# All of w_down's product by seven products: z's factors kept split in DRAM, and some weights' rests made by adding DMAs

## The chip, the cores and the metric

The kernel runs on one core of a Trainium2 chip. The metric is device microseconds (us) of one execution. The kernel before was timed three times: median 1957.88 us, 1957.66 to 1958.37. TensorE (PE) multiplies into PSUM banks; VectorE (DVE), ScalarE (ACT) and GpSimd (POOL) do the rest; SyncE (SP) issues most of the DMAs, ACT's queue some.

## The reference

One layer of a hybrid streaming encoder, 512 positions of 2048 channels, float32:

```python
u = rms_norm(h, mix_pre_gain)
p = u @ w_in                      # 2048 x 5120, two convolution branches follow
o = concat(y_a, y_b) @ w_out      # 2048 x 2048
h = h + rms_norm(o, mix_post_gain)
m = rms_norm(h, mlp_pre_gain)
z = square(relu(m @ w_up))        # 2048 x 8192
z = z @ w_down                    # 8192 x 2048
h = h + rms_norm(z, mlp_post_gain)
```

The change touches the last two products, the MLP.

## The kernel before

**Precision.** A float32 operand is split into a high part (rounded to fp32r by ACT) and a rest (value minus high part, by DVE). A product of two such operands takes three matmuls: high x rest, rest x high, high x high.

**Products by seven.** A 2 x 2 block product is made from seven block products instead of eight, with sums of blocks on either side (Strassen's scheme in Winograd's form). In the code `r11`, `r21`, `r22` are plain blocks of the activation side, `t1` to `t4` sums of them; on the weight side `n11`, `n12`, `n21`, `n22` are blocks and `s1` to `s4` sums, made on DVE from freshly loaded raw weights.

**Weights.** The class `Stationary` (lines 109 to 254) keeps an ordered list of jobs, one for each 128 x 1024 piece. A job loads raw pieces on SP's queue into 6 `raw` buffers, adds or subtracts where it is a sum, then makes the high part (line 237, ACT) and the rest (line 242, DVE) into two of 43 `slot` buffers of 4 KB a partition, which most things share; the oldest free one is taken. `take(n, ahead)` prepares jobs `ahead` of the ones used. Raw loads are issued in order when a job that frees a raw buffer is done, `W.ahead` = 5 sources further on.

**The first MLP product** (lines 766 to 860): eight of the 64 output tiles of w_up plainly, then 28 pairs of tiles by `by_seven` (line 361). Each of a pair's seven products has 24 matmuls of 256 columns into a bank of its own, of seven that rotate. Work on the result is put in `pending` and issued in the next product, behind the preparation of weights (`run_pending` after `W.take`). After a pair, ACT makes Relu and Square and stores z to DRAM (`relu_squared`, line 766).

**The second MLP product** (lines 863 to 1019): w_down's 64 row blocks in eight chunks of eight, the result in column tiles of 512. z is the stationary side (128 x 128 blocks), weights move, 512 columns a matmul (`wide`, lines 882 to 884). In each of seven chunks, two column tiles are made plainly (`wide_tile`, four token banks of 8 blocks each) and two by seven (`wide_seven`), their results added up in SBUF by DVE (line 335, through `accumulate`). z comes back from DRAM and is split there; for the sums it is loaded again, subtracted and split (`strassen_sums`). The last chunk is made plainly for all four tiles, its second half by token block at the end, so that the norm's sums and the output follow block by block. There `turn` transposes h back on PE (line 999).

The order of work is written out by hand: each engine issues in program order, and waits are semaphores that follow from the data and from the reuse of buffers.

## Time and profile before

| | |
|---|---|
| median of three runs | 1957.88 us |
| profiled execution | 1959.29 us, its span 1957.6 us |
| busy: PE, DVE, ACT, POOL | 99%, 78%, 42%, 4% |
| first MLP product by sevens, in the window 750 to 1277 us | PE busy throughout, DVE 403.56 of 527 us |
| w_down product, in the window 1420 to 1856 us | PE busy throughout, DVE 346.57 of 436 us |
| DMA over the span | 272.54 MB, 139 GB/s |

The span goes from the first to the last instruction. Busy time is the union of an engine's instructions; matmuls are pipelined, so the duration of one is longer than the step from one to the next. Rows of groups show line, engine, operation, output and inputs by the program's names, shape and count, then busy us and mean ns, then the idle time before them and what ended it.

### The profile page before, as it was taken

What the parts mean: (1) busy time and instruction counts of PE and PEld (TensorE: products, weight loads), DVE (VectorE), ACT (ScalarE), POOL (GpSimd) and SP (SyncE); (2) the same over time, 40 slices, a digit from 0 to 9 for tenths busy, and PEclk for the clock granted to TensorE, in tenths of its full rate; (3) what the DMA queues carried; (4) which work ended last, traced back from release to release, by engine and by line L of the source; (5) the groups of instructions that cost most, each with busy time, mean ns of one, the idle gap of its engine ahead of it and who ended that gap; (6) DMA issues with size and microseconds to landing.
All of it is one profiled execution on the core that took longest, in us unless ns stands there. A gap on an engine that the chain in (4) does not pass through costs nothing.

```text
span 1957.6 us, 28019 instructions
## 1 busy us (share of the span) xinstructions
PE 1936.3 (99%) x11218; PEld 1716.1 (88%) x11218; DVE 1522.6 (78%) x2000; ACT 815.9 (42%) x1102; POOL 75.4 (4%) x70
## 2 busy tenths in 40 slices
PE   8999999999999999999999999999999999999998
PEld 6888888888999789999999999988888888888876
DVE  8799989667785787777777777776687777877748
ACT  6222112252443745454444545446243343433442
POOL 4000010300210000000000000000000000000000
PEclk9999999999999999999999999999999999999999
DMA  7232323232346724343343434446253363533632
GB/s 250 83 113 95 108 87 108 86 107 76 117 153 227 253 81 159 111 137 133 116 155 108 158 112 135 147 171 235 84 197 130 129 219 102 195 127 132 237 107 87
DMA packets 85523, 272.54 MB, mean 139 GB/s; under 512 B 9616, under 2 KB 11792, under 8 KB 85392
## 3 DMA queue, kind: packets, MB, share of 16 engines
q1 hardware_dynamic: 71568, 245.92, 38.1%
q10 hardware_dynamic: 13824, 24.82, 3.3%
q8 instruction: 88, 1.44, 0.3%
q14 instruction: 43, 0.35, 0.1%
HBM read 241.87 MB, written 28.84 MB: 138 GB/s over the span
## 4 chain that ended last, share of the span: by engine, by line
PE 96%; DVE 2%; DMA 1%; ACT 1%; issue 0%; SPq 0%; ACTq 0%; DVEq 0%
PE bank L296 57%; PE bank L882 11%; PE bank L883 11%; PE bank L884 11%; PE bank L315 2%; PE bank L316 2%; PE bank L314 2%; DVE slot L242 1%; DMA tmp<-x_in 1%; PE bank L999 0%; DVE slot L98 0%; PE sums L383 0%; DVE slot L1077 0%; DMA raw<-w_in_in 0%; DMA par_sb<-par_in 0%
## 5 line engine op out<-in xcount | busy, mean ns | idle before, releaser
L296 PE MATMUL bank<-slot,slot 128*128 128x256 f32 (+1 forms) x7584 | 1127.6, 311 | 0.0
L296 PEld LDWEIGHTS bank<-slot,slot 128*128 128x128 f32 x7584 | 1047.0, 191 | 80.1 <-issue 1.4
L242 DVE TENSOR_TENSOR slot<-raw,slot 128x1024 fp32r<-128x1024 f32 x332 | 410.6, 1255 | 61.7 <-ACT slot L237 55.4
L237 ACT ACTIVATE slot<-raw 128x1024 fp32r<-128x1024 f32 x332 | 338.1, 1049 | 134.0 <-DVE raw L212 67.4
L882 PE MATMUL bank<-slot,slot 128*128 128x512 f32 x968 | 378.1, 391 | 0.8
L883 PE MATMUL bank<-slot,slot 128*128 128x512 f32 x968 | 376.7, 389 | 0.2 <-DVE slot L95 0.2
L884 PE MATMUL bank<-slot,slot 128*128 128x512 f32 x968 | 376.7, 389 | 0.0
L237 ACT ACTIVATE slot<-slot 128x1024 fp32r<-128x1024 f32 x170 | 176.9, 1057 | 285.3 <-PE bank L296 161.7
L242 DVE TENSOR_TENSOR slot<-slot,slot 128x1024 fp32r<-128x1024 f32 x170 | 210.7, 1240 | 56.9 <-PE bank L882 41.8
L882 PEld LDWEIGHTS bank<-slot,slot 128*128 128x128 f32 x968 | 181.7, 188 | 40.8 <-ACT tmp L1002 3.3
L883 PEld LDWEIGHTS bank<-slot,slot 128*128 128x128 f32 x968 | 181.7, 188 | 37.8 <-DVE slot L95 0.5
L884 PEld LDWEIGHTS bank<-slot,slot 128*128 128x128 f32 x968 | 181.7, 188 | 37.8
L335 DVE TENSOR_TENSOR tmp<-tmp,bank 128x256 f32<-128x256 f32 x224 | 93.9, 419 | 113.5 <-PE bank L296 112.4
L94 ACT ACTIVATE slot<-tmp 128x512 fp32r<-128x512 f32 x96 | 54.1, 607 | 274.1 <-DVE tmp L335 153.4
L501 DVE SCALAR_TENSOR_TENSOR slot<-slot,par_sb,slot 128x512 f32<-128x512 f32 x240 | 163.0, 746 | 0.0
L335 DVE TENSOR_TENSOR slot<-slot,bank 128x512 f32<-128x512 f32 x164 | 105.8, 682 | 19.1 <-PE bank L884 19.1
L95 DVE TENSOR_TENSOR slot<-slot,slot 128x512 fp32r<-128x512 f32 (+1 forms) x80 | 49.7, 660 | 48.4 <-ACT slot L94 48.4
L314 PE MATMUL bank<-slot,slot 128*128 128x512 f32 (+1 forms) x216 | 81.1, 375 | 6.2 <-ACT slot L94 6.2
L316 PE MATMUL bank<-slot,slot 128*128 128x512 f32 (+1 forms) x216 | 81.0, 375 | 2.9 <-DVE slot L98 2.9
L95 DVE TENSOR_TENSOR slot<-tmp,slot 128x512 fp32r<-128x512 f32 x96 | 60.3, 666 | 29.6 <-ACT slot L94 29.4
L315 PE MATMUL bank<-slot,slot 128*128 128x512 f32 (+1 forms) x216 | 80.9, 374 | 1.8 <-DVE slot L242 1.8
L165 DVE TENSOR_TENSOR slot<-raw,raw 128x1024 f32<-128x1024 f32 x64 | 78.0, 1219 | 0.0
(98 smaller groups left out, 936.4 us busy)
## 6 DMA issues: line engine op xcount, KB each, us to landing
raw<-w_up_in SPq DMA_DIRECT2D x128, 512.0 KB, 5.2
raw<-w_down_in SPq DMA_DIRECT2D x128, 512.0 KB, 4.6
raw<-w_in_in SPq DMA_DIRECT2D x76, 512.0 KB, 4.4
slot<-z_dram SPq DMA_DIRECT2D x60, 512.0 KB, 6.5
raw<-w_out_in SPq DMA_DIRECT2D x32, 512.0 KB, 4.3
z_dram<-tmp ACTq DMA_DIRECT2D x64, 256.0 KB, 5.4
tmp<-x_in SPq DMA_DIRECT2D x16, 256.0 KB, 5.2
slot<-x_in SPq DMA_DIRECT2D x8, 512.0 KB, 8.7
```

Source lines behind the costliest of these rows:

```text
L95: nc.vector.tensor_tensor(lo, value, hi.bitcast(F32), op=ALU.subtract)
L237: nc.scalar.activation(hi, value, AF.Copy)
L242: nc.vector.tensor_tensor(lo, value, hi.bitcast(F32), op=ALU.subtract)
L296: nc.tensor.matmul(ps, s, m, start=n == 0, stop=n == len(todo) - 1)
L314: nc.tensor.matmul(ps[:, cols], hi, mhi, start=first, stop=False)
L315: nc.tensor.matmul(ps[:, cols], lo, mhi, start=False, stop=False)
L316: nc.tensor.matmul(ps[:, cols], hi, mlo, start=False, stop=last)
L335: add = lambda out, a, b, op=ALU.add: nc.vector.tensor_tensor(out, a, b, op=op)
L501: nc.vector.scalar_tensor_tensor(out=acc, in0=g[:, k : k + S], scalar=w, in1=acc, op0=ALU.mult, op1=ALU.add)
L882: nc.tensor.matmul(ps, z_hi, lo, start=first, stop=False)
L883: nc.tensor.matmul(ps, z_lo, hi, start=False, stop=False)
L884: nc.tensor.matmul(ps, z_hi, hi, start=False, stop=last)
```

## The change

All four column tiles of w_down's product are now made by seven in each of the seven chunks, two `wide_seven` calls a chunk in place of two plain tiles and one call. Products that share a term go on in the same PSUM bank: the three of `p6`, the two of `p5` and the two of `p1` each have a pair of banks, which DVE reads between them. What belongs to three of the four quarters (`p1`) is added up once in `shared` and put into them near the end.

z's parts and sums are made in the first product, by steps (`z_jobs`) of which one goes along with each product (two where more than eight wait): Relu, Square and high part; store and rest; store and the sums t1 to t4; their high part; store and rest; store. Parts lie in DRAM by factor, so that the second product loads ready factors (`load_factor`) and splits nothing. Stores have rows of 1 KB, four a partition; a factor's load has rows of 4 KB.

`by_seven` makes its products in the order r11, t2, t1, r21, t3, r22, t4; r21 goes on in r11's bank and t4 in t3's, with a sign turned in t4. DVE makes five additions a pair instead of seven, and ACT one more copy.

One weight piece a pair in w_up and two a unit in w_down get their rest without DVE: ACT writes the negated high part, and a DMA that POOL issues adds the raw weights to it from DRAM. w_down's units load in another order, their `12` pieces into slots.

The diff at its core ("..." where lines are left out; removed lines are shown only in `prepare`, `product` and `by_seven`):

```diff
+            self.jobs.append((lambda: self.get(n), n + 1, None))
+        def strassen(self, even, odd, added_up=False):
+            def sub(out, a, b, op=ALU.subtract):
+                nc.vector.tensor_tensor(out, a, b, op=op)
+                return out
             def p6():
+                s["1"], s["2"] = slot([P, WCOLS]), slot([P, WCOLS])
+                sub(s["1"], self.get(n21), self.get(n22), ALU.add)
+                return sub(s["2"], s["1"], self.get(n11))
+            def p7():
+                return sub(self.get(n11), self.get(n11), self.get(n21))
+            for value, frees, added in (
+                (lambda: self.get(n11), 0, None),
+                (p6, 0, None),
+                (lambda: s["1"], 0, None),
+                (lambda: self.get(n12), 0, None),
+                (p7, 2, None),
+                (lambda: sub(s["2"], self.get(n12), s["2"]), 0, None),
+                (lambda: self.get(n22), 4, odd[1] if added_up else None),
+                self.jobs.append((value, n11 + frees if frees else 0, added))
...
         def strassen_wide(self, units):
+            n, s, last = {}, {}, {}
+            for name in ("21a", "22a", "21b", "22b", "11a", "11b"):
                 n[name] = self.source(units[name])
+            first = n["21a"]
...
             def raw(name):
+                return self.get(n[name])
             def s1(u):
                 s[u] = slot([P, WCOLS])
+                return sub(s[u], raw("21" + u), raw("22" + u), ALU.add)
             def s2(u):
+                last[u] = slot([P, WCOLS])
+                nc.sync.dma_start(last[u], units["12" + u])
+                return sub(s[u], s[u], raw("11" + u))
+            for value, frees, added in (
+                (lambda: s1("a"), 0, None),
+                (lambda: s1("b"), 0, None),
+                (lambda: s2("a"), 0, None),
+                (lambda: s2("b"), 0, None),
+                (lambda: raw("11a"), 0, None),
+                (lambda: raw("11b"), 0, None),
+                (lambda: sub(raw("11a"), raw("11a"), raw("21a")), 2, None),
+                (lambda: sub(raw("11b"), raw("11b"), raw("21b")), 4, None),
+                (lambda: sub(s["a"], last["a"], s["a"]), 0, None),
+                (lambda: sub(s["b"], last["b"], s["b"]), 0, None),
+                (lambda: raw("22a"), 5, units["22a"]),
+                (lambda: raw("22b"), 6, units["22b"]),
+                (lambda: last["a"], 0, None),
+                (lambda: last["b"], 0, None),
+                self.jobs.append((value, first + frees if frees else 0, added))
...
         def prepare(self, upto):
             while len(self.parts) < upto:
                 while len(self.high) < min(len(self.parts) + 2, len(self.jobs)):
-                    value = self.jobs[len(self.high)][0]()
+                    value, _, added = self.jobs[len(self.high)]
+                    value = value()
                     hi, lo = slot([P, WCOLS], F32R), None
                     nc.scalar.activation(hi, value, AF.Copy)
+                    if added is not None:
+                        lo = slot([P, WCOLS], F32R)
+                        nc.scalar.activation(lo, hi.bitcast(F32), AF.Copy, scale=-1.0)
+                        nc.gpsimd.dma_start(lo, added, accum_op=ALU.add)
                     self.high.append((value, hi, lo))
                 value, hi, lo = self.high[len(self.parts)]
                 if lo is None:
                     lo = slot([P, WCOLS], F32R)
-                nc.vector.tensor_tensor(lo, value, hi.bitcast(F32), op=ALU.subtract)
+                    nc.vector.tensor_tensor(lo, value, hi.bitcast(F32), op=ALU.subtract)
...
     for m in range(UP_PLAIN, N_UP, 2):
+        W.strassen(w_up[m], w_up[m + 1], True)
     for c in range(N_CHUNK - 1):
+        for _ in range(N_WIDE // 2):
+            W.strassen_wide({name: w_down[next(down_units)] for name in SEVEN_UNITS})
+    def products(ps, blocks, at=None, f=None, onto=False):
...
+            nc.tensor.matmul(
+                ps, s, m, start=n == 0 and not onto, stop=n == len(todo) - 1, skip_group_check=onto
+            )
...
-    def product(right, blocks):
+    def product(right, blocks, onto=None):
         (part,) = W.take(1, 3)
         run_pending()
-        ps = bank(TOK)
-        products(ps, [(block(part, i), right(i)) for i in range(blocks)])
+        ps = bank(TOK) if onto is None else onto
+        products(ps, [(block(part, i), right(i)) for i in range(blocks)], onto=onto is not None)
         return ps
     def by_seven(product, c1, c2, done1, done2, step=lambda n: None):
-        p1, u = scratch(TOK), scratch(TOK)
-        evacuate(nc.scalar.activation, p1, product("r11"), AF.Copy)
+        p1, u, v = scratch(TOK), scratch(TOK), scratch(TOK)
+        first = product("r11")
+        evacuate(nc.scalar.activation, p1, first, AF.Copy)
         evacuate(add, u, p1, product("t2"))
-        p5 = product("t1")
-        evacuate(add, c1[:, upper], u, p5)
-        evacuate(add, c1[:, lower], p1, product("r21"))
-        evacuate(add, u, u, product("t3"))
-        evacuate(add, c2[:, upper], u, p5)
+        evacuate(add, v, u, product("t1"))
+        product("r21", first)
+        evacuate(nc.scalar.activation, c1[:, lower], first, AF.Copy)
+        seventh = product("t3")
+        evacuate(add, c2[:, upper], v, seventh)
         evacuate(step, 1)
-        evacuate(add, c2[:, lower], u, product("t4"), ALU.subtract)
+        evacuate(add, c1[:, upper], v, product("r22"))
+        evacuate(done1, c1)
+        evacuate(step, 3)
+        product("t4", seventh)
+        evacuate(add, c2[:, lower], u, seventh)
         evacuate(done2, c2)
-        evacuate(step, 3)
-        evacuate(add, c1[:, upper], c1[:, upper], product("r22"))
-        evacuate(done1, c1)
...
+    FACTORS = ("r11", "r12", "r21", "r22", "t1", "t3", "t2", "t4")
+    WIDE_ORDER = ("t1", "t2", "r11", "t3", "r22", "t4", "r21")
+    PAIRS = CHUNK // 2
+    z_dram = dram.tile([P, N_UP // 2 * 16 * TOK], F32, name="z_dram")
+    z_parts = z_dram.rearrange(
+        "p (c g f h i w) -> c g h i p f w", g=2, f=4, h=2, i=PAIRS, w=TOK
+    )
+    z_jobs = deque()
+    def keep_z(n, zt):
+        c, i = divmod(n, PAIRS)
+        made = {}
+        def squared():
+            nc.scalar.activation(zt, zt, AF.Relu)
+            nc.scalar.activation(zt, zt, AF.Square)
+            high(zt, 0)
+        def high(value, g):
+            made["hi", g] = slot([P, 4, TOK], F32R)
+            nc.scalar.activation(
+                made["hi", g].rearrange("p f w -> p (f w)"),
+                value.rearrange("p a b -> p (a b)"), AF.Copy,
+            )
+        def rest(value, g):
+            made["lo", g] = slot([P, 4, TOK], F32R)
+            add(
+                made["lo", g].rearrange("p f w -> p (f w)"),
+                value.rearrange("p a b -> p (a b)"),
+                made["hi", g].rearrange("p f w -> p (f w)").bitcast(F32), ALU.subtract,
+            )
+        def store(g, h):
+            part = made["lo" if h else "hi", g]
+            nc.scalar.dma_start(z_parts[c, g, h, i], part.bitcast(F32))
+        def sums():
+            t = made["t"] = slot([P, 4, TOK])
+            q = zt.rearrange("p a (b w) -> p (a b) w", b=2)
+            add(t[:, :2, :], q[:, 1::2, :], q[:, :2, :], ALU.subtract)
+            add(t[:, 2, :], q[:, 3, :], t[:, 0, :], ALU.subtract)
+            add(t[:, 3, :], q[:, 2, :], t[:, 2, :], ALU.subtract)
+        z_jobs.append([squared])
+        z_jobs.append([lambda: store(0, 0), lambda: rest(zt, 0)])
+        if c == N_CHUNK - 1:
+            z_jobs.append([lambda: store(0, 1)])
+            return
+        z_jobs.append([lambda: store(0, 1), sums])
+        z_jobs.append([lambda: high(made["t"], 1)])
+        z_jobs.append([lambda: store(1, 0), lambda: rest(made["t"], 1)])
+        z_jobs.append([lambda: store(1, 1)])
+    def z_job(n):
+        for _ in range(min(n, len(z_jobs))):
+            pending.extend(z_jobs.popleft())
...
+    def plain_z(n, pss, zt):
+        for i, ps in enumerate(pss):
+            nc.scalar.activation(zt[:, i, :], ps, AF.Copy)
+        keep_z(n, zt)
...
+    def up_product(name, onto=None):
+        z_job(2 if len(z_jobs) > 8 else 1)
+        return product(right_factor[name], HALF, onto)
+    factors = {}
+    def load_factor(c, name):
+        f = FACTORS.index(name)
+        for h in range(2):
+            t = factors[c, name, h] = slot([P, PAIRS, TOK], F32R)
+            nc.sync.dma_start(
+                t.rearrange("p i w -> p (i w)").bitcast(F32),
+                z_dram.rearrange("p (n w) -> n p w", w=PAIRS * TOK)[((c * 2 + f // 4) * 4 + f % 4) * 2 + h],
+            )
+    def load_first(n):
+        for name in WIDE_ORDER[3 * (n == 3) : 3 + (n == 3)]:
+            load_factor(0, name)
...
     for m in range(UP_PLAIN, N_UP, 2):
+        zt = slot([P, 2, S])
         by_seven(
             up_product,
+            zt[:, 0, :],
+            zt[:, 1, :],
+            lambda c: None,
+            lambda c, m=m, zt=zt: keep_z(m // 2, zt),
+            load_first if m == N_UP - 2 else lambda n: None,
+        )
+    total, shared = {}, {}
...
+    def right_blocks(c, name, i):
+        return [factors[c, name, h][:, i, :] for h in range(2)]
...
+    def wide_seven(c, t, after):
+        if c == 0:
+            for name in ((t, 0), (t, 1), (t + 1, 0), (t + 1, 1), None):
+                pair = slot([P, 2, WIDE])
+                if name is None:
+                    shared[t] = pair
+                else:
+                    for j in range(2):
+                        total[name[0], 2 * name[1] + j] = pair[:, j, :]
...
+        banks = {}
+        for q, (name, group, to, first) in enumerate((
+            ("t1", "p5", "c2 upper", True),
+            ("t2", "p6", "c1 upper", True),
+            ("r11", "p1", "all but c1 lower", True),
+            ("t3", "p6", "c2 upper", False),
+            ("r22", "p5", "c1 upper", False),
+            ("t4", "p6", "c2 lower", True),
+            ("r21", "p1", "c1 lower", True),
+        )):
+            z_job(1)
+            parts = W.take(2, 4)
+            run_pending()
+            if group not in banks:
+                banks[group], onto = [bank() for _ in range(2)], False
+            else:
+                onto = True
+            for j, ps in enumerate(banks[group]):
+                for i in range(PAIRS):
+                    wide(
+                        ps, right_blocks(c, name, i), j, parts[i // 2], i % 2,
+                        i == 0 and not onto, i == PAIRS - 1, True,
+                    )
+                evacuate(accumulate, c == 0 and first, sums[to][j], ps)
+            after(q)
+    run_pending()
+    for name in WIDE_ORDER[4:]:
+        load_factor(0, name)
+    for c in range(N_CHUNK - 1):
+        following = WIDE_ORDER if c < N_CHUNK - 2 else FACTORS[:4]
+        def after(q):
+            if q > 0 and q - 1 < len(following):
+                load_factor(c + 1, following[q - 1])
+        for t in range(0, N_WIDE, 2):
+            wide_seven(c, t, after if t == 2 else lambda q: None)
+        if len(following) == len(WIDE_ORDER):
+            load_factor(c + 1, following[-1])
...
```

More of the change, by code (lines that the diff above doesn't have):

```diff
@@ L870, in accumulate @@
             add(to, to, ps)
-    def new_total(t):
-        for n in range(TB // 2):
-            pair = slot([P, 2, WIDE])
-            for i in range(2):
-                total[t, 2 * n + i] = pair[:, i, :]
-    def wide(ps, z_hi, z_lo, part, n, first, last):
-        hi, lo = (w[:, n * WIDE : (n + 1) * WIDE] for w in part)
-        nc.tensor.matmul(ps, z_hi, lo, start=first, stop=False)
-        nc.tensor.matmul(ps, z_lo, hi, start=False, stop=False)
-        nc.tensor.matmul(ps, z_hi, hi, start=False, stop=last)
@@ L886, in encoder_block, with wide @@
-    tokens = lambda n: slice(n * P, (n + 1) * P)
-    def wide_tile(t, first_sum, blocks, make_moving, step=lambda: None, ahead=4):
+    tokens = lambda n: slice(n * P, (n + 1) * P)
+    def wide(ps, right, b, part, n, first, last, onto=False):
+        hi, lo = (w[:, n * WIDE : (n + 1) * WIDE] for w in part)
+        z_hi, z_lo = (t[:, tokens(b)] for t in right)
+        matmul = lambda a, b, first=False, last=False: nc.tensor.matmul(
+            ps, a, b, start=first, stop=last, skip_group_check=onto
+        )
+        matmul(z_hi, lo, first=first)
+        matmul(z_lo, hi)
+        matmul(z_hi, hi, last=last)
@@ L890, in wide_tile @@
+    def wide_tile(t, c, blocks, step):
         pss = [bank() for _ in range(TB)]
         for n in range(0, len(blocks), 2):
-            (part,) = W.take(1, ahead)
+            (part,) = W.take(1, 4)
             run_pending()
             for i in range(2):
-                moving = make_moving(blocks[n + i])
                 for b, ps in enumerate(pss):
                     wide(
-                        ps, *both(moving, tokens(b)), part, i,
+                        ps, plain_block(c, blocks[n + i], b), b % 2, part, i,
@@ L902, in wide_tile @@
         for b, ps in enumerate(pss):
-            evacuate(accumulate, first_sum, total[t, b], ps)
-    def wide_seven(c):
-        if c == 0:
-            for _ in range(7):
-                seven.append(slot([P, 2, WIDE]))
-        for q, name in enumerate(("r10", "t10", "t11", "t20", "t21", "r21", "r20")):
-            parts = W.take(2, 4)
-            run_pending()
-            n, half = int(name[1]) - 1, int(name[2]) * TB // 2
-            right = lambda i: z[c * CHUNK + 2 * i + n] if name[0] == "r" else t_z[i][n]
-            for j in range(2):
-                ps = bank()
-                for i in range(CHUNK // 2):
-                    wide(
-                        ps, *both(right(i), tokens(half + j)), parts[i // 2], i % 2,
-                        i == 0, i == CHUNK // 2 - 1,
-                    )
-                evacuate(accumulate, c == 0, seven[q][:, j, :], ps)
-            if q > 1:
-                z_step(3)
```

177 lines of the change are left out of this document (36 added, 141 removed).

## Prediction

> **What bounds the kernel now.** I read the page's busy times, then TensorE's waits, then the stages.
>
> ```profile
> PE 1936.3 (99%) x11218; PEld 1716.1 (88%) x11218; DVE 1522.6 (78%) x2000; ACT 815.9 (42%) x1102; POOL 75.4 (4%) x70
> PE 96%; DVE 2%; DMA 1%; ACT 1%; issue 0%; SPq 0%; ACTq 0%; DVEq 0%
> ```
>
> ```profile
> PE bank L314 <- ACT slot L94: 6.2, 1, 6.2
> PE bank L316 <- DVE slot L98: 2.9, 4, 0.9
> PE bank L315 <- DVE slot L242: 1.8, 1, 1.8
> PE bank L883 <- DVE slot L95: 0.2, 1, 0.2
> ```
>
> TensorE (PE) is busy for 99% of the span, makes 96% of the chain that ended last, and waits about 11 us in all, nearly all of it ahead of the MLP. Time therefore goes where matmuls go, as long as the other engines keep up. How near they are is read by stage: first the h stage, then the first MLP product by sevens, then the w_down product. Columns: window, its us, then busy us of PE, PEld, DVE, ACT, POOL, the granted clock, the DMA engines' share, GB/s.
>
> ```profile
> 610.00:671.00 61.00, 58.13 (x358) 51.89 (x358) 49.48 (x89) 34.19 (x56) 0.00 (x0) 1.00 0.72 254
> 750.00:1277.00 527.00, 527.00 (x4394) 527.00 (x4393) 403.56 (x469) 254.06 (x312) 0.00 (x0) 1.00 0.41 135
> 1420.00:1856.00 436.00, 436.00 (x1925) 361.04 (x1924) 346.57 (x453) 167.67 (x207) 0.62 (x2) 1.00 0.47 161
> ```
>
> In both stages that the change rewrites PE never idles and VectorE (DVE) is busy for 77% and 79%. It is the engine that could take over.
>
> **Term 1, matmuls removed.** The w_down product's first and last step, the transposes between, and two equal points of successive pairs in the first MLP product:
>
> ```profile
> L882 PE MATMUL bank<-slot,slot x968: 389/389/501, 1279.5 to 1947.3; 128*128 128x512 f32 x194
> L999 PE MATMUL bank<-tmp,slot 128*128 128x128 f32 x64 | 8.3, 272 | 0.0
> 1000.38 0.37 ACT L343 ACTIVATE tmp<-bank 128x256 f32<-128x256 f32 x1
> 1020.53 0.36 ACT L343 ACTIVATE tmp<-bank 128x256 f32<-128x256 f32 x1
> ```
>
> Lines 882 to 884 have 968 each, 2904 in all, so from the first to the last start there are 2903 steps. (667.8 - 8.3) / 2903 = 0.227 us a matmul; the 0.389 us are a pipelined duration, and taking them would overstate the gain. A chunk before: two wide tiles of 8 blocks x 4 token banks x 3 = 192, and seven products of 2 banks x 4 blocks x 3 = 168; together 360. After: 2 x 168 = 336. 24 fewer in each of seven chunks are 168, x 0.227 = **-38.2 us**. The first product keeps 168 matmuls a pair, 20.15 us a pair, 2.88 us for each of its seven products; a product of the second takes 24 x 0.227 = 5.45 us.
>
> **Term 2, the first product's 28 pairs.** They hide all the new z work, so the cover has to be counted. Groups of this stage, and others of the page for single forms:
>
> ```profile
> L242 DVE TENSOR_TENSOR slot<-slot,slot 128x1024 fp32r<-128x1024 f32 x103 | 125.5, 1219 | 0.0
> L335 DVE TENSOR_TENSOR tmp<-tmp,bank 128x256 f32<-128x256 f32 x184 | 77.3, 420 | 106.7 <-PE bank L296 105.8
> L335 DVE TENSOR_TENSOR tmp<-slot,slot 128x512 f32<-128x512 f32 x16 | 11.1, 692 | 0.8
> L237 ACT ACTIVATE slot<-raw 128x1024 fp32r<-128x1024 f32 x80 | 83.8, 1049 | 12.4 <-PE bank L296 12.4
> L343 ACT ACTIVATE tmp<-bank x32: 360/364/366, 520.1 to 1262.5; 128x256 f32<-128x256 f32 x32
> L769 ACT ACTIVATE tmp<-tmp 128x512 f32<-128x512 f32 x52 | 32.9, 633 | 1.7
> 998.98 0.33 ACTq L770 DMA_DIRECT2D z_dram<-tmp  x1
> ```
>
> DVE before, a pair: 11 operations of 1024 (7 rests, 4 sums) x 1.22 + 7 evacuations x 0.42 = 16.4; the window shows 403.56 / 26.15 pairs = 15.4, since neighbours overlap (factor 0.94). After: 10 x 1.22 + 5 x 0.42 for weights and banks, 2 x 1.22 for z's rests, 0.69 + 2 x 0.42 for its sums: 18.3, x 0.94 = 17.2 of 20.15 us (85%). ScalarE (ACT): 254.06 / 26.15 = 9.7, plus a negated copy 1.05, a bank copy 0.36, two z copies 2.10, Relu and Square on 1024 for 512 (-0.4), two more DMA issues 0.7: 13.5 us (67%). Neither exceeds PE, so the base case costs nothing, but DVE's idle time falls from 4.7 to 2.9 us a pair.
>
> Two new waits lie inside. The fourth product goes on in the first's bank after ACT has copied it, with two products (5.8 us) in between. The seventh goes on in the fifth's bank, and DVE must have read that within one product, 2.88 us. Behind the third product's evacuation DVE has z's sums (1.5), two weight sums and two rests (4 x 1.22), then this read: 0.4 + 1.5 + 4.9 + 0.4 = 7.2 us after the third product's end; the seventh starts 3 x 2.88 = 8.6 after it. Margin 1.4 us: enough, if nothing ahead of that read waits.
>
> What can wait is a slot. The right factors hold 28 of the 43, and a pair takes 22 from the other 15, so one is reused one to two products after its release. A z part is released by its store's landing. DMA rows, KB and median us to landing, then the z stores' and z loads' spread:
>
> ```profile
> raw<-w_up_in SPq DMA_DIRECT2D x128, 512.0 KB, 5.2
> raw<-w_down_in SPq DMA_DIRECT2D x128, 512.0 KB, 4.6
> z_dram<-tmp ACTq DMA_DIRECT2D x64, 256.0 KB, 5.4
> slot<-x_in SPq DMA_DIRECT2D x8, 512.0 KB, 8.7
> raw<-w_in_in SPq DMA_DIRECT2D x16, 128.0 KB, 4.0
> DMA to landing us min/median/max: 2.0/5.5/9.4
> GB/s 424 416 414 360 212 113 301 185 395 419 338 21 11 0 0 0 0 67 274 124 277 336 376 359 398 416 407 403 402 306 290 201 211 317 226 285 215 298 185 172
> ```
>
> By my count the next write into the first rest's slot comes about 5.2 us after its store starts. Landing at 5.4 costs nothing beyond the margin; at 9.4 it costs 9.4 - 5.2 - 1.4 = 2.8 us a pair, 78 us. The bytes argue for the near end: nine transfers of 0.524 MB a pair are 4.72 MB in 20.15 us, 234 GB/s, against 5 x 0.524 = 130 before, and the h stage reached 424. A store with rows of 1 KB isn't in the trace; the w_in pieces with such rows (4.0 us for a quarter of the bytes) put it between 4 and 16 us, nearest to 6. I take **+3 us** (0 to 60).
>
> At the stage's start the eight plain tiles leave four pairs of z, 24 z steps, worked off two to a product: the first pair's DVE gets 14 steps for 6, 14 / 6 x 3.7 + 13.5 + 8 late rests x 0.42 = 25.5 us against 20.15. Weights made three products ahead (8.6 us) cover most of it: **+2 us** (0 to 9).
>
> **Term 3, the adding DMAs.** One a pair, two a w_down unit; no such DMA and no DMA from POOL is in the trace, and POOL has nothing else to do there (0.00 above). The hi copy and its negation are issued in the third product, the rest is needed by the seventh: 4 x 2.88 = 11.5 us, less two copies, leaves 9.4 for the landing. Bounds: 5.2 (the same bytes loaded) and 10.4 (source and destination each cost a load). I take 7, nearer to the plain load, and so **0 us** (0 to 28 x 1.0 = 28). In w_down three products, 16.4 us, lie between. What it spares is one DVE rest, in term 2 already. Without it DVE would be at 91%.
>
> While POOL works, a DVE subtract of 1.22 us can take twice as long:
>
> ```profile
> 27.03 2.32 DVE L242 TENSOR_TENSOR slot<-raw,slot 128x1024 fp32r<-128x1024 f32 x1
> 26.40 1.87 POOL L408 TENSOR_TENSOR sum<-sum,tmp 128x512 f32<-128x512 f32 x1 [1.71 <-ACT tmp L412]
> ```
>
> At 1.1 us a DMA this would be 1.1 of DVE's 2.9 idle us a pair, still hidden. [...]
>
> **Term 4, the w_down product.** DVE before, a chunk (360 x 0.227 = 81.8 us of PE):
>
> ```profile
> L335 DVE TENSOR_TENSOR slot<-slot,bank 128x512 f32<-128x512 f32 x120 | 77.2, 683 | 12.3 <-PE bank L884 12.3
> L95 DVE TENSOR_TENSOR slot<-slot,slot 128x512 fp32r<-128x512 f32 x48 | 31.0, 687 | 25.1 <-ACT slot L94 25.1
> SPq L122 <- DVE raw L212: 236.4, 14, 30.0
> ```
>
> 30 weight operations x 1.22, 22 bank additions x 0.68, z's 16 rests x 0.69 and 16 sums x 0.42: 69 us, the window shows 65. After: 40 x 1.22 + 28 x 0.68 = 67.8, x 0.94 = 64 of 76.3 us (84%). Bytes: 20 weight transfers and 14 factors are 17.8 MB, 234 GB/s. SP issues 30 DMAs a chunk for 24, in one order; loads wait there for buffers already (236 us), and a factor that waits for PE now holds back the weights queued behind it. The last raw load of a unit (11b) is asked for only when its sum is next, so DVE waits a load of 4.6 us once a unit, of its 6.2 idle us there. Weights are ready about two products (10.9 us) ahead. **+3 us** (0 to 42, rival 3). A bank is gone on with one product after its read is due, as before by rotation: nothing.
>
> **Term 5, the seam.**
>
> ```profile
> 1269.76 9.64 PE L296 MATMUL bank<-slot,slot 128*128 128x256 f32 x79
> 1279.45 0.50 PE L882 MATMUL bank<-slot,slot 128*128 128x512 f32 x1
> ```
>
> PE passes from one product to the other without a gap. After, it needs two factors whose loads are issued around the last pair's sixth product, behind at most a few raws: **+1 us** (0 to 6). The end (12 additions for 14) changes nothing that PE waits for.
>
> **Sum.** -38.2 + 3 + 2 + 0 + 3 + 1 = -29.2. The span of 1957.6 becomes 1928.4. The profiled execution took 1959.29, 1.4 above the median of 1957.88; on the median the forecast is **1928.7 us**.
>
> **Rivals.** (1) *Stores hold the slots.* If a z store lands at 7.5 us, DVE's fifth-bank read is late by 7.5 - 5.2 - 1.4 = 0.9 us, and PE waits in each pair: 28 x 0.9 = 25 in place of term 2's 3, 1951 us. For it: no slot is spare, DVE at 85%. Against: z stores of half the size land at 5.4, with DMA engines far from full. (2) *Slower: the adding DMA is late* in the first product. Every us beyond 9.4 costs 28; it undoes the gain from 9.4 + 38.2 / 28 = 10.8 us on. At 12, 73 us: 1928.7 + 73 = 2002 us. For it: it must read and write the same bytes. Against: four products of cover. (3) *The SP queue starves w_down.* A factor waiting one product (5.45) ahead of 11b makes DVE's wait 10; less 6.2 idle and some of the lead, 3 us a unit, 14 units, 42: 1968 us. For it: SP's long waits now. Against: PE never waited through them.
>
> **Chances.** Forecast, PE bound with under 20 us of waits: 57%, own range 1918 to 1940. Rival 1: 18%, rival 2: 15%, rival 3: 10%. 0.2%, about what this measurement can tell, is 4 us. Faster: 57 + 13 of rival 1 + 3 of rival 3 = 73%; same: 5 + 2 = 7%; slower: 15 + 5 = 20%. The range runs from all covers holding and the seam free, 1916, to rival 3, 1970.
>
> **What would show it.** 2736 wide matmuls at 0.227 us; pairs still 20.15 us apart; DVE about 85% in both stages; z stores landing under 6.6 us and adding DMAs under 9.4. It is wrong if PE's waits name the bank line in the first product with ACT or DVE or a POOL DMA behind it, or the wide matmuls with a weight's rest behind it, for over 20 us.

## The result: 3.7% slower

The changed kernel takes 2029.84 us (median of four runs, 2024.50 to 2034.29), the kernel before 1957.77 us beside it: ratio 1.0365, 95% interval 1.0352 to 1.0378. The forecast of 1928.7 us and its range, up to 1970, are missed, and with them the sign. The profiled execution took 2024.5 us with a span of 2022.8, so the span grew by 65.2 us.

From the page after, the busy times:

```profile
PE 1919.6 (95%) x11050; PEld 1696.6 (84%) x11050; DVE 1563.1 (77%) x1932; ACT 914.3 (45%) x1114; POOL 129.6 (6%) x126
```

PE makes 168 matmuls fewer, as planned, but idles for 2022.8 - 1919.6 = 103 us, 21 before. Its busy time fell by 16.7 us only: taking away 38.2 leaves 21.5 us by which the remaining matmuls keep it busy longer. DVE, at 77%, is no busier than it was (78%). So no engine ran out of time; PE stands and waits. PE's waits after (waiting line, what released it; us in total, times, longest us):

```profile
PE bank L299 <- DMA slot<-w_up_in: 33.6, 24, 2.6
PE bank L299 <- ACT slot L237: 15.1, 2, 10.0
PE bank L299 <- DVE slot L340: 13.8, 2, 12.5
PE bank L935 <- DVE slot L340: 11.6, 5, 2.9
PE bank L935 <- ACT slot L925: 4.9, 1, 4.9
PE bank L299 <- ACT tmp L348: 2.0, 1, 2.0
```

Line 299 is the first MLP product, line 935 the wide matmuls of w_down; a slot filled from `w_up_in` by a DMA is a rest made by adding (line 241). Line 299 waiting for ACT, DVE and POOL's DMA, for over 20 us, is what the prediction had named as its refutation. By stage, first the first MLP product before, then after (window, its us, busy us of PE, PEld, DVE, ACT and POOL, granted clock, DMA share, GB/s), then after's wide matmuls with their first and last start:

```profile
671.00:1279.50 608.50, 608.45 (x4899) 600.71 (x4897) 462.20 (x561) 298.60 (x381) 0.00 (x0) 1.00 0.40 133
```

```profile
671.00:1358.40 687.40, 622.93 (x4892) 609.86 (x4891) 518.09 (x622) 383.31 (x434) 24.50 (x28) 0.97 0.69 205
```

```profile
L935 PE MATMUL bank<-slot,slot x2736: 387/389/792, 1358.4 to 2013.6; 128*128 128x512 f32 x196
```

The first product takes 78.9 us more. The w_down product takes 655.2 us from its first to its last start, 667.8 before: 12.6 less, that is -38.2 for its removed matmuls and +25.6 of new loss. What follows the last matmul is 1.1 us shorter. 78.9 - 12.6 - 1.1 = 65.2.

**The first product splits once more.** PE's timeline after, stretches without a stop: start, us, and at the end in brackets the stop ahead of the stretch and its releaser. A pair's seven products are 168 matmuls, 20.15 us when undisturbed:

```profile
745.28 22.49 PE L299 MATMUL bank<-slot,slot 128*128 128x256 f32 x168 [12.45 <-DVE slot L340]
777.74 21.76 PE L299 MATMUL bank<-slot,slot 128*128 128x256 f32 x169 [9.97 <-ACT slot L237]
825.57 23.10 PE L299 MATMUL bank<-slot,slot 128*128 128x256 f32 x168 [5.09 <-ACT slot L237]
872.07 20.42 PE L299 MATMUL bank<-slot,slot 128*128 128x256 f32 x168 [1.59 <-DMA slot<-w_up_in]
916.16 21.91 PE L299 MATMUL bank<-slot,slot 128*128 128x256 f32 x168 [1.94 <-DMA slot<-w_up_in]
...
1310.70 20.42 PE L299 MATMUL bank<-slot,slot 128*128 128x256 f32 x168 [2.63 <-DMA slot<-w_up_in]
...
1354.05 4.49 PE L299 MATMUL bank<-slot,slot 128*128 128x256 f32 x23 [2.02 <-DMA slot<-w_up_in]
```

From 872.07 to 1354.05 are 22 pairs of 21.91 us: 1.76 more than before in each, 38.7 in all, with one stop a pair on the adding DMA. The other 40 us lie in the pairs ahead of these, in long stops on ACT and DVE and in slow stretches behind them (granted clock 0.80 from 745 to 757 us, 0.72 from 825 to 837).

**How a steady pair stops.** The timeline around the third product of one pair:

```profile
1099.16 1.05 ACT L790 ACTIVATE slot<-slot 128x1024 f32<-128x1024 f32 x1
1100.24 1.06 ACT L791 ACTIVATE slot<-slot 128x1024 f32<-128x1024 f32 x1
1101.34 1.06 ACT L796 ACTIVATE slot<-slot 128x1024 fp32r<-128x1024 f32 x1
1102.30 1.04 ACT L237 ACTIVATE slot<-raw 128x1024 fp32r<-128x1024 f32 x1
1103.38 1.06 ACT L240 ACTIVATE slot<-slot 128x1024 fp32r<-128x1024 f32 x1
1104.85 0.86 POOL L241 DMA_DIRECT2D slot<-w_up_in  x1 [20.84 <-DVE slot L340]
1105.42 1.22 DVE L163 TENSOR_TENSOR slot<-raw,raw 128x1024 f32<-128x1024 f32 x1
...
1110.39 0.41 DVE L340 TENSOR_TENSOR slot<-tmp,bank 128x256 f32<-128x256 f32 x1
...
1113.45 2.78 PE L299 MATMUL bank<-slot,slot 128*128 128x256 f32 x21 [1.31 <-DMA slot<-w_up_in]
```

The seventh product was due at 1113.45 - 1.31 = 1112.14, so the third began 4 x 2.88 earlier, at 1100.6. But the copy of the last weight (line 237) comes only at 1102.30: ACT has z's Relu, Square and high part (lines 790, 791, 796) ahead of it in its order. POOL issues at 1104.85, which leaves 7.3 us to 1112.14. (The bracket of POOL's row names a DVE operation that ended shortly before; but in each of the last 20 pairs POOL issues 0.41 us after the end of the negated copy, line 240, whatever DVE did, so that copy is what it follows.) The DMA groups of the page (count, KB, median us to landing):

```profile
raw<-w_up_in SPq DMA_DIRECT2D x128, 512.0 KB, 4.5
z_dram<-slot ACTq DMA_DIRECT2D x120, 512.0 KB, 5.9
slot<-w_up_in POOLq DMA_DIRECT2D x28, 512.0 KB, 8.6
slot<-w_down_in POOLq DMA_DIRECT2D x28, 512.0 KB, 8.5
```

8.6 against 7.3 is the 1.3 us by which PE stands.

**How a w_down unit stops.** SP's, DVE's and PE's rows around the end of one chunk, then DVE's wait over seven chunks:

```profile
1540.62 78.11 PE L935 MATMUL bank<-slot,slot 128*128 128x512 f32 x336 [2.87 <-DVE slot L340]
...
1590.20 1.23 SPq L900 DMA_DIRECT2D slot<-z_dram  x2
1591.52 0.38 SPq L207 DMA_DIRECT2D slot<-w_down_in  x1
1591.95 0.42 SPq L122 DMA_DIRECT2D raw<-w_down_in  x1
1600.89 1.23 DVE L195 TENSOR_TENSOR slot<-slot,raw 128x1024 f32<-128x1024 f32 x1 [8.22 <-DMA raw<-w_down_in]
...
1620.38 76.58 PE L935 MATMUL bank<-slot,slot 128*128 128x512 f32 x336 [1.66 <-DVE slot L340]
```

```profile
DVE slot L195 <- DMA raw<-w_down_in: 63.7, 14, 9.4
```

DVE waits 8.22 us for 11b, which SP asked for at 1591.95 behind two factors and another piece. Later in the chunk it reads a bank late (line 340), and PE stops. A chunk takes 1620.38 - 1540.62 = 79.8 us instead of 76.3.

### The profile page after: what moved, and what is told of

Its sections match the earlier page's. It is cut to its first block, busy times and chain, and to the rows that moved or that the text cites. A ratio compares the mean times of both kernels' runs of the same rounds, so it can differ in the third digit from the quotient of the medians.

```text
span 2022.8 us, 28179 instructions
## 1 busy us (share of the span) xinstructions
PE 1919.6 (95%) x11050; PEld 1696.6 (84%) x11050; DVE 1563.1 (77%) x1932; ACT 914.3 (45%) x1114; POOL 129.6 (6%) x126
## 4 chain that ended last, share of the span: by engine, by line
PE 29%; DMA 16%; DVE 8%; issue 6%; ACT 4%; SPq 0%; ACTq 0%; DVEq 0%; POOLq 0%
PE bank L935 24%; DMA z_dram<-slot 7%; DMA slot<-w_up_in 6%; PE bank L299 4%; DVE slot L246 2%; DMA raw<-w_down_in 2%; DVE slot L340 2%; ACT slot L237 2%; DVE slot L163 1%; DVE slot L195 1%; DMA raw<-w_up_in 1%; ACT slot L791 1%; ACT slot L790 1%; ACT slot L796 0%; DVE raw L163 0%
## 5 line engine op out<-in xcount | busy, mean ns | idle before, releaser
L935 PE MATMUL bank<-slot,slot 128*128 128x512 f32 x2736 | 631.3, 392 | 19.3 <-DVE slot L340 11.6
L237 ACT ACTIVATE slot<-slot 128x1024 fp32r<-128x1024 f32 x208 | 218.9, 1057 | 382.9 <-DVE slot L195 211.1
L246 DVE TENSOR_TENSOR slot<-raw,slot 128x1024 fp32r<-128x1024 f32 x280 | 349.8, 1263 | 46.1 <-ACT slot L237 40.5
L246 DVE TENSOR_TENSOR slot<-slot,slot 128x1024 fp32r<-128x1024 f32 x208 | 254.1, 1222 | 60.4 <-PE bank L299 23.3
L340 DVE TENSOR_TENSOR slot<-slot,slot 128x1024 fp32r<-128x1024 f32 (+2 forms) x128 | 104.7, 824 | 102.2 <-DMA z_dram<-slot 47.9
L340 DVE TENSOR_TENSOR slot<-slot,bank 128x512 f32<-128x512 f32 x208 | 133.9, 680 | 27.8 <-PE bank L935 27.8
L195 DVE TENSOR_TENSOR slot<-slot,raw 128x1024 f32<-128x1024 f32 x28 | 34.3, 1225 | 78.2 <-DMA raw<-w_down_in 77.7
L241 POOL DMA_DIRECT2D slot<-w_up_in x28 | 24.5, 875 | 717.2 <-DVE slot L340 399.5
L796 ACT ACTIVATE slot<-slot 128x1024 fp32r<-128x1024 f32 x60 | 63.4, 1056 | 12.7 <-DVE slot L340 9.7
L417 POOL TENSOR_TENSOR sum<-sum,tmp 128x512 f32<-128x512 f32 x35 | 59.4, 1698 | 94.5 <-ACT tmp L421 93.3
L240 ACT ACTIVATE slot<-slot 128x1024 fp32r<-128x1024 f32 x56 | 59.4, 1060 | 1.8
L241 POOL DMA_DIRECT2D slot<-w_down_in x28 | 24.4, 870 | 527.8 <-ACT slot L240 375.5
```

The lines of the kernel that those rows point to most:

```text
L237: nc.scalar.activation(hi, value, AF.Copy)
L240: nc.scalar.activation(lo, hi.bitcast(F32), AF.Copy, scale=-1.0)
L246: nc.vector.tensor_tensor(lo, value, hi.bitcast(F32), op=ALU.subtract)
L340: add = lambda out, a, b, op=ALU.add: nc.vector.tensor_tensor(out, a, b, op=op)
L417: nc.gpsimd.tensor_tensor(self.total, self.total, t, op=ALU.add)
L796: nc.scalar.activation(made["hi", g].rearrange("p f w -> p (f w)"), value.rearrange("p a b -> p (a b)"), AF.Copy,)
```

## The experiments

The theory after these readings: the price is paid by three separate lateness chains, the last weight's job in a w_up pair, the bunched z steps at the start of that stage, and 11b in w_down. The rivals: the larger DMA traffic or the busier DVE slows the kernel as a whole; the stores of z hold the slots; the shared banks cost by themselves. In all results below the kernel before ran beside, at 1959.0 to 1959.4 us; ratios are to it. Savings are differences of medians, uncertain by the 1.5 us between those runs and the first ones. Each kernel ran four times, the one with `by_seven` alone ten times.

### Each suspected chain alone

No adding DMA in the first product (DVE makes all rests there):

```diff
-        W.strassen(w_up[m], w_up[m + 1], True)
+        W.strassen(w_up[m], w_up[m + 1])
```

> The first MLP product's adding DMAs are left out: DVE makes all seven rests of a pair, as before the change. Theory A (the adding DMA lands about 1.5 us after the seventh product wants it, in each steady pair): the pairs go from 21.9 back to about 20.2 us, PE's waits on that DMA (33.6 us) are gone, and the time falls by 35 to 42 us, to about 1992 us. Rival (DVE at 91% is then the limit, or the stores' slots are): pairs stay above 21.5 us with PE waiting on DVE or ACT, and the time changes by less than 10 us.

Measured: 1972.18 us, ratio 1.0070 (1.0055 to 1.0085), 57.7 less than the changed kernel and more than the steady pairs' 38.7. PE's timeline and a window of it:

```profile
837.17 163.08 PE L299 MATMUL bank<-slot,slot 128*128 128x256 f32 x1349 [1.02 <-DVE slot L340]
```

```profile
872.07:1300.00 427.93, 427.76 (x3546) 426.32 (x3546) 383.15 (x435) 241.96 (x273) 0.00 (x0) 1.00 0.66 204
```

PE runs without a stop through these pairs, although DVE now has one more rest a pair and is busy for 383 / 428 = 90%. The DMA engines still move 204 GB/s there. So DVE's load does not stop PE, and rival 1 is no first cause, since every z store is still made. Of the profiled executions' difference, 54.4 us, 38.7 belong to the steady pairs, about 13 to the stretch ahead of 872 us and about 3 to w_down. Ahead of 872 us, too, the changed kernel has long stops on line 237, a weight's copy on ACT.

w_down's 11b asked for earlier (the number in a job says up to which source loads are asked for once its rest is made):

```diff
-                (lambda: raw("22b"), 6, units["22b"]),
+                (lambda: raw("22b"), 7, units["22b"]),
```

> In a w_down unit the last raw load (11b of the next unit) is asked for when 22b's piece is done, not when DVE needs it. Theory C (DVE waits 8 to 9 us for that load once a chunk, works off the delay for 30 us and reads PE's banks 2.4 us late at the chunk's end): DVE's waits on w_down loads (63.7 us) fall under 15, PE's waits at the chunk boundaries go, and the time falls by 12 to 20 us, to about 2014 us. Rival (DVE is late by its own load of 85%, or by slots): the waits at the boundaries stay and the time changes by less than 4 us.

Measured: 2014.42 us, ratio 1.0282 (1.0267 to 1.0298), 15.4 less. PE's stops at the chunks' ends are gone:

```profile
1390.14 510.13 PE L935 MATMUL bank<-slot,slot 128*128 128x512 f32 x2242 [3.78 <-ACT slot L925]
```

The other 10 of the 25.6 us lost in w_down, then, belong to the seam in front of this stretch.

Twelve of the z steps that wait at the stage's start are made already beside its last plain tiles:

```diff
     for m in range(START, UP_PLAIN):
+        if m > START:
+            z_job(4)
```

> Twelve of the 24 z steps that wait at the start of the pairs are worked off along with the last three plain tiles, four to a tile. Theory B (the backlog of z steps in the first four pairs makes ACT and DVE late, which costs about 40 us with the lower granted clock after the stops): the stops of 12.5 and 10 us shrink to less than half, and the time falls by 18 to 35 us, to about 2003 us. Rival (the stops come from slots held by stores and by the late sums, whatever the number of steps): less than 8 us.

Measured: 2011.82 us, ratio 1.0269 (1.0254 to 1.0284), 18.0 less. The stops of 12.45 and 9.97 us shrink to a few us but do not vanish, and the one ahead of them grows from 2.01 to 4.59:

```profile
742.20 23.10 PE L299 MATMUL bank<-slot,slot 128*128 128x256 f32 x168 [3.86 <-DVE slot L340]
768.34 21.87 PE L299 MATMUL bank<-slot,slot 128*128 128x256 f32 x168 [3.03 <-ACT slot L237]
```

### What about the adding DMA is too dear

Its start moved: the copy, the negated copy and the DMA are issued one job earlier.

```diff
+        def begin(self, n):
+            if n not in self.begun:
...
+                self.begun[n] = value, hi, lo
+            return self.begun[n]
...
+                    self.high.append(self.begin(len(self.high)))
+                    for n in range(len(self.high), min(len(self.high) + 1, len(self.jobs))):
+                        if self.jobs[n][2] is not None:
+                            self.begin(n)
```

> High part, negation and adding DMA of a piece are issued one job earlier; nothing else changes. Theory A (the DMA only starts too late): PE's waits on it in the first product (33.6 us) fall under 8 and the time falls by 30 to 42 us, to about 1994 us. Rival (what starts it late is ACT and DVE, blocked by slots that z stores hold; two slots more for a product make that worse): less than 10 us gained, or slower, with more waits of ACT and DVE on the z stores.

Measured: 2023.44 us, ratio 1.0329 (1.0312 to 1.0346): only 6.4 less. PE's wait on the DMA is gone, but another has its place (PE's timeline, then DVE's wait; line 349 is here what 340 is in the changed kernel, line 805 what 796 is, z's high part):

```profile
947.54 20.42 PE L308 MATMUL bank<-slot,slot 128*128 128x256 f32 x168 [0.75 <-DVE slot L349]
968.71 20.42 PE L308 MATMUL bank<-slot,slot 128*128 128x256 f32 x168 [0.75 <-DVE slot L349]
```

```profile
DVE slot L349 <- ACT slot L805: 51.0, 21, 2.7
```

A pair still takes 968.71 - 947.54 = 21.17 us. With the two weight copies ahead of z's high part, DVE waits for that part, and its later bank reads are late. So the theory as far as it blamed the landing alone fell: moving the one thing forward on ACT makes the other late.

ACT's negated copy kept, the DMA left out; DVE writes the rest over the copy (first product only):

```diff
-                        nc.gpsimd.dma_start(lo, added, accum_op=ALU.add)
+                        if len(self.high) < self.down:
+                            lo = (lo,)
+                        else:
+                            nc.gpsimd.dma_start(lo, added, accum_op=ALU.add)
...
-                if lo is None:
-                    lo = slot([P, WCOLS], F32R)
+                if lo is None or isinstance(lo, tuple):
+                    lo = slot([P, WCOLS], F32R) if lo is None else lo[0]
```

> As the changed kernel, but in the first product ACT's negated high part is written and then overwritten by DVE's rest: the negation and its slot stay, the DMA goes. With the DMA issued a job earlier PE no longer waited for it and the pairs still took 21.2 us. Theory A1 (the rest of the loss is ACT's negation, 1.05 us ahead of z's steps, that makes DVE read the fifth's bank late): pairs above 20.9 us and PE waiting on DVE. Theory A2 (it needs the DMA): pairs at 20.2 to 20.4 us and a time near 1972, as with the adding DMA left out.

Measured: 1993.00 us, ratio 1.0172 (1.0157 to 1.0187).

```profile
946.82 20.39 PE L303 MATMUL bank<-slot,slot 128*128 128x256 f32 x168 [0.73 <-DVE slot L344]
968.01 20.39 PE L303 MATMUL bank<-slot,slot 128*128 128x256 f32 x168 [0.80 <-DVE slot L344]
```

The pairs take 968.01 - 946.82 = 21.19 us, and PE stops on DVE, as theory A1 has it. But the rows of the same pair name another wait (line 240 is the negated copy, 249 a weight's rest):

```profile
958.55 1.06 ACT L240 ACTIVATE slot<-slot 128x1024 fp32r<-128x1024 f32 x1
959.65 1.23 DVE L249 TENSOR_TENSOR slot<-raw,slot 128x1024 fp32r<-128x1024 f32 x1 [0.81 <-ACT slot L240]
```

z's high part stands ahead of the negated copy here, as it does in the changed kernel. DVE writes the rest over that copy and so waits for it, 0.81 us, about as long as PE then stops; between 872 and 1300 us these waits sum to 17.1 us in 21 pairs. In the kernel with neither copy nor DMA the same DVE operations follow each other without a wait and PE runs through; the changed kernel makes no such rest on DVE. The 20.8 us over the 1972.18 of the kernel with neither are therefore mainly the price of a wait that this experiment brought in. What the negated copy alone costs in the changed kernel is not shown by it, nor is theory A1.

z's steps moved instead: every pair's steps come one product later, so that ACT makes the last weight's two copies ahead of Relu, Square and the high part. Adding DMAs stay.

```diff
-            lambda c, m=m, zt=zt: keep_z(m // 2, zt),
+            lambda c, m=m, zt=zt: (z_jobs.append([]), keep_z(m // 2, zt)),
```

> The changed kernel with every z step of the pairs one product later, so that ACT makes the last weight's high part and negation ahead of Relu, Square and z's high part, not behind them. If these 3.2 us of z copies are what starts the adding DMA late (7.3 us are left for a landing of 8.6): PE's waits on it (33.6 us) fall under 10 and the pairs come to 20.2 to 21.2 us, 20 to 45 us faster than the changed kernel. If the DMA itself is too slow whenever it starts: the waits stay and the time is within 8 us.

Measured: 1984.05 us, ratio 1.0139 (1.0122 to 1.0156), 45.8 less with not one instruction taken away. PE's timeline:

```profile
846.21 466.86 PE L299 MATMUL bank<-slot,slot 128*128 128x256 f32 x3887 [0.36 <-DMA slot<-w_up_in]
```

All steady pairs run through. In one of these pairs POOL issues at 978.94, which leaves 8.6 us to the seventh product's start at 987.59, where 7.3 were left above; the median landing is 7.9 here. This settles the steady pairs: neither the DMA nor the negated copy costs anything there where ACT's order suits them.

### The chains together, and what remains

The first three edits at once:

> The three single edits together: no adding DMA in the first product, 11b asked for early, twelve z steps along with the plain tiles. If the three costs lie in different places and add up (57.7 measured with the first alone, 15.4 with the second, 18.0 with the third): 2029.8 - 91.1 = 1938.7 us, faster than before by 1%, pairs at 20.2 us. If leaving the adding DMA out already removed part of what the others remove (the granted clock after stops, the first pairs): 1945 to 1957 us.

Measured: 1944.70 us, ratio 0.9923 (0.9908 to 0.9938). The three savings sum to 91.1 us and would give 1938.7; they overlap by 6.

The same without w_down's adding DMAs:

```diff
-                (lambda: raw("22a"), 5, units["22a"]),
-                (lambda: raw("22b"), 7, units["22b"]),
+                (lambda: raw("22a"), 5, None),
+                (lambda: raw("22b"), 7, None),
```

> As the three edits together, and DVE makes all rests of w_down too: no adding DMA is left, four DVE operations more a chunk, DVE at about 90% of 76.3 us. If the adding DMAs also cost time in w_down (ACT's negation, 8.5 us to landing): 3 to 10 us faster than the three edits. If they are covered there by the three products that lie between: within 3 us of it, or slower by up to 10 where DVE then reads the banks late.

Measured: 1942.40 us, ratio 0.9915 (0.9900 to 0.9929), not to be told from the one before: in w_down the adding DMAs cost and gain nothing that shows.

The three edits, six z steps a plain tile in place of four, and the last job of each w_up pair asks for one source more, so that at the seam w_down's first 11b is asked for earlier:

```diff
-                (lambda: self.get(n22), 4, odd[1] if added_up else None),
+                (lambda: self.get(n22), 5, odd[1] if added_up else None),
...
+            z_job(6)
```

> As the three edits together, but six z steps a plain tile in place of four, and the last raw load ahead of the seam (the first unit's 11b, for which DVE waits 10.4 us there) asked for one source earlier. If the first pairs' remaining stops come from the backlog and the seam's stops from that load: PE's stops in the first pairs fall under 6 us and those at the seam (7.4 us) under 3, 6 to 14 us faster than the three edits. If ACT's own work in the plain tiles or the factor loads at the seam set them: within 3 us of it.

Measured: 1941.94 us, ratio 0.9913 (0.9897 to 0.9930). The groups, windows and PE's timeline of this run:

```profile
L937 PE MATMUL bank<-slot,slot x2736: 387/389/501, 1298.9 to 1930.1; 128*128 128x512 f32 x196
```

```profile
931.00:1298.00 367.00, 366.82 (x3042) 365.67 (x3042) 327.37 (x372) 208.41 (x235) 0.00 (x0) 1.00 0.67 207
1330.00:1838.00 508.00, 508.00 (x2243) 420.61 (x2242) 413.26 (x441) 226.32 (x226) 23.18 (x28) 1.00 0.74 239
671.00:1298.90 627.90, 613.83 (x4890) 604.38 (x4890) 550.53 (x653) 352.94 (x409) 0.00 (x0) 0.99 0.65 200
```

```profile
747.15 183.94 PE L299 MATMUL bank<-slot,slot 128*128 128x256 f32 x1512 [6.91 <-DVE slot L340]
```

w_down takes 631.2 us from first to last start, 36.6 less than before, of 38.2 that its removed matmuls make. PE never stops in the w_down window, with DVE at 81%, nor to speak of in the steady pairs, with DVE at 89%. The first product is still 627.9 - 608.5 = 19.4 us longer than before, with 14.1 us of PE's idle time in it; half of that is one stop of 6.91. The forecast of 6 to 14 us was missed, 2.8 measured: the seam's stops fell from 7.4 us to 1.0, but those ahead of and in the first pairs grew from 9.6 us with four steps a tile to 14.1.

This kernel without any adding DMA:

> As the kernel with six z steps a plain tile and the seam's load asked for earlier (1941.9 us, wide matmuls over 631 us where 629.6 is 2736 x 0.227 and the transposes), without the adding DMAs in w_down too. If they are fully covered in w_down: within 2 us of it, 1940 to 1944. If they still cost there: 1936 to 1939. If DVE at 90% is late at the banks without them: over 1946.

Measured: 1940.51 us, ratio 0.9910 (0.9895 to 0.9925), the same.

And with never more than one z step a product:

```diff
-        z_job(2 if len(z_jobs) > 8 else 1)
+        z_job(1)
```

> As the kernel with six z steps a plain tile and the seam's load, but never more than one z step to a product, so that what is left of the backlog spreads over more pairs. If two steps a product overload DVE in the first pair (its stop of 6.9 us): that stop falls under 3 us and the time by 3 to 6 us, to about 1937. If slots that wait for z are what stops it, which longer-held z tiles make worse: the same or up to 5 us slower.

Measured: 1942.10 us, ratio 0.9916 (0.9901 to 0.9931). The edit changed nothing: where 18 of the 24 steps are worked off beside the plain tiles, never more than eight wait, so the doubling is never reached, and ACT, DVE and POOL run the same operations in the same order in both traces. The forecast was thus not tried, and what makes the stop of 6.91 us stays open. In the trace DVE works without a pause from 737.0 us until its bank read at 746.59, for which PE waits; the read stands there behind z's rest and sums, two rests of the right factors' late sums and five weight operations.

The kernel before with nothing but the new order of products and the shared banks of `by_seven`:

> The kernel before with the new products by seven alone: their new order, the two shared banks, five DVE additions instead of seven, weights' sums in place. z and w_down as before. If the shared banks cost nothing while DVE has 4 us or more idle a pair: within 2 us of before. If going on in a bank stops PE by itself: PE waits for DVE or ACT in each pair, 28 x 0.8 = 22 us slower.

Measured: 1958.47 us, ratio 0.9998 (0.9989 to 1.0008). Going on in a bank costs nothing of itself, and the two evacuations spared bring nothing, as long as PE bounds.

The kernel with these edits and its variant without any adding DMA, at about 1941 us, beat both the kernel before, by 0.9%, and the changed one, by 4.4% (1 - 0.9913 / 1.0365). They are alike within their intervals.

## Why the prediction was wrong

**What bounds the kernel; term 1.** Right. Matmuls bound the kernel wherever nothing else is late, and the removed ones are worth what was summed: -36.6 measured in the repaired w_down against -38.2.

**Term 3, the step that failed.** The overlap was counted wrong: "less two copies, leaves 9.4 for the landing" starts at the third product as if ACT were free then. ACT has 3.2 us of z's work of the same product ahead of the copies. In the pair shown that work runs 1.7 us into the third product, and POOL issues 0.4 us after the second copy, so 7.3 us were left. The landing itself, 8.6 us, lies inside the bounds of 5.2 to 10.4, though past the 7 taken, and would have met the 9.4: with the z steps behind the copies, PE stops only once, for 0.36 us. Rival 2 had the mechanism, at the wrong threshold: the gain was undone not from a landing of 10.8 us on, but at 8.6. In w_down term 3 was right at 0.

**Term 2, the steady pairs.** Right for the changed kernel. The load was sized well: DVE 89% measured with all rests on it, where "91%" stood for that case. In the pair shown, DVE's read of the fifth's bank ends at 1110.80, 7.3 us after the third product's end at 1103.5, where 7.2 was forecast, and 1.3 us before the seventh product was due, where the margin was to be 1.4. That margin held only "if nothing ahead of that read waits", and the sole wait looked for was a slot. The experiment with the DMA a job earlier shows another: z's rest waits 2.71 us for ACT's high part in place of 1.40 where both weight copies stand ahead of it, and PE stops 0.75 us a pair. Rival 1 is not the cause: stores landed at 5.9 us, under its 6.6. DVE did wait for slots that they held (40.9 us between 872 and 1300 us), but PE's stops there, 27.8 us, name the adding DMA alone, and the pairs ran through without that DMA, and with the z steps later, though both kernels make all of the stores.

**Term 2, the stage's start.** Mis-sized: 2 us (0 to 9) for about 40. The estimate summed DVE's work over a pair against a lead of three products. But z's steps alternate between ACT and DVE, each waiting for the other within a step, and weights are made by the same two engines in between; an engine's busy share says nothing of that. Between 716 and 860 us DVE waited 11.3 us for z's high parts, ACT 9.7 us for z's sums, and ACT's weight copies 26.0 us for DVE's weight sums. Moving half the steps ahead gave 18.0 back, leaving the adding DMAs and their copies out about 13 in this stretch; 14 us of idle time stay even with both, and their cause is open.

**Term 4.** The wait for 11b was named, at 4.6 us less 6.2 idle; it was 8.22, as rival 3 supposed, which expected 10 and 42 us in all. The rows put the delay in the load's landing behind the two factors and a piece asked for 1.8 us earlier, not in SP's queue. It cost 15.4 us.

**Term 5.** 1 us (0 to 6) for stops of 1.92 and 4.92 us, of which 0.60 and 0.39 remain once 11b is asked for earlier.

**The clock, no term at all.** The 21.5 us by which PE's remaining matmuls keep it busy longer have two parts. One is the granted clock. In this trace it is 1.00 or 0.50; from 700 us to the last matmul it is 0.50 in seven stretches, each 3.41 us long or two, three or four times that, and they begin whole multiples of 3.41 us apart. Three windows of after, then the sum over the seven stretches:

```profile
913.70:917.11 3.41, 1.47 (x13) 1.27 (x12) 0.04 (x1) 2.79 (x3) 0.00 (x0) 1.00 0.61 187
917.11:920.52 3.41, 3.41 (x19) 3.41 (x18) 3.41 (x4) 0.00 (x0) 0.00 (x0) 0.50 0.40 136
1306.23:1309.64 3.41, 1.84 (x16) 1.64 (x14) 3.41 (x5) 0.00 (x0) 0.00 (x0) 1.00 0.66 135
```

```profile
sum 47.78, PE 29.45 PEld 27.58 DVE 33.58 ACT 25.61 POOL 2.89; mean PE 4.21 PEld 3.94 DVE 4.80 ACT 3.66 POOL 0.41
```

PE is busy for 29.45 us at a clock of 0.50. In one stretch of 3.41 us it loses 1.5 us when busy throughout: 21.91 - 20.42 = 1.49 for the pair from 916.16, 78.11 - 76.58 = 1.53 for the chunk from 1540.62. Matmuls of 256 columns begin 0.213 us apart there instead of 0.120, those of 512 columns 0.427 instead of 0.227. By these rows 29.45 / 3.41 x 1.5 = 13.0 us, an estimate; before, the clock was 0.50 for one stretch with PE busy, 1.5 by the same estimate. That leaves 11.5 of the 21.5. The other part is the end of the last matmul ahead of each stop, which otherwise lies under the next one: 168 matmuls between two stops keep PE busy for 20.42 us, where a pair's step is 20.15. An estimate from these rows, 29 stops on line 299 x 0.27 and 7 on line 935 x (0.39 - 0.23), gives 9.0 us. The two make 20.5; the last 1.0 is open.

Which stop lowers the clock in this trace depends on where it falls. The one of 1.94 us ahead of 916.16 lies wholly inside one stretch of 3.41 us, in which PE is busy for 1.47, and the next stretch has half the clock. The one of 2.63 us ahead of 1310.70 is shared by two stretches, PE is busy for 1.84 us in the first, and the clock stays full. From 700 us on, every stretch at full clock in which PE idled for 1.94 us or more was followed by one at half, and none in which it idled for 1.80 or less. So 1.94 us of idle time within one such stretch were enough here, and a prediction should price short stops too.

**The range.** Its low end of 1916 us does not follow from its own words: all covers holding and the seam free is 1957.9 - 38.2 = 1919.7. Nothing else hung on it.

## What to carry to other kernels

Work moved to an engine with idle time is not free: find where it stands in that engine's order, what lies behind it there, who waits for that and with what margin. A busy share cannot tell this; here DVE at 90% stopped nobody, and ACT at 56% of a stage stopped PE in every pair. When a new job and an old one share an in-order engine, try exchanging them before taking either away: one product's shift of the z steps was worth 46 us.

## What the runs showed of the hardware

A DMA that adds 512 KB from DRAM into a slot took 8.6 us to land (median of 28, 8.5 in w_down), where loading the same bytes took 4.5. POOL was busy for 0.86 us with issuing one; a DVE operation of 1024 elements right beside it took its usual 1.22 us, so the doubling to 2.32 that the prediction weighed did not occur (1104.85 and 1105.42 in the timeline of one pair). Of 55 DVE operations that ran beside such an issue for 0.3 us or more, none took over 1.02 times the median of its group.

Stores with rows of 1 KB landed in 5.9 us for 512 KB, beside 5.4 for half as many bytes before. After a stop of 1.94 us that lay wholly inside one stretch of 3.41 us the granted clock was 0.50 for the next 3.41 us: matmuls of 256 columns began 0.213 us apart in that stretch, 0.120 in the one behind it.
